# The sample's state updates as a stream of their own, behind its outputs, in a decoder layer on one core

## The chip, the cores and the metric

The kernel runs on one NeuronCore of a Trainium2 chip. The metric is the device time of one execution in microseconds (us); the median of three runs is compared, and the trace is of one profiled execution. The engines are named as in the profile: PE (TensorE, products), DVE (VectorE), ACT (ScalarE), POOL (GpSimd) and SP (SyncE, which issues the DMAs here).

## The reference

One decoder layer for 512 prompt tokens and for a sample of 8 sequences with 4 new tokens each. Its three parts are a half-step feed-forward network, a mixer and a second feed-forward network. All of it is in float32. The mixer, cut to what matters here:

```python
def token_mixer(h, pos, conv_buf, S0, attend, p):
    proj = h @ p['w_in']
    u, z, b_raw, a_raw, q_sw, k_sw, v_sw, gate_a, gate_b = jnp.split(proj, split_idx, axis=-1)
    ...
    o_dn, S_new = gated_delta_rule(q_dn, k_dn, v_dn, g, beta, S0)
    o_dn = rmsnorm(o_dn, p['dn_norm']) * jax.nn.silu(z)
    ...
    y = jax.nn.sigmoid(gate_a) * o_dn + jax.nn.sigmoid(gate_b) * o_sw
    return y @ p['w_out'], (kbuf_new, vbuf_new, conv_new, S_new)

def step(S, xs):                      # gated_delta_rule, one chunk
    v_new = un - jnp.einsum('bhcd,bhde->bhce', wn, S)
    o = (jnp.einsum('bhcd,bhde->bhce', qn * jnp.exp(gn)[..., None], S)
         + jnp.einsum('bhij,bhje->bhie', an, v_new))
    S = S * jnp.exp(g_last)[..., None] + jnp.einsum('bhcd,bhce->bhde', k_dec, v_new)
    return S, o
```

So a chunk of the delta rule gives an output `o`, from the old state, and a new state. The output goes through a norm (the inverse root of its mean square) and a gate and is added to the attention's output; the state goes to memory. Each of the 8 heads has a state of 128 x 128 floats for the prompt and eight of them, one per sequence, for the sample.

## The kernel before

The 544 tokens (512 + 32) are worked on as two halves of 272. A float32 product is made of three products of rounded parts (line 301): hi x hh, hi x hl and lo x hh, where hi and lo are the two parts of a weight block (line 270 casts hi on ACT, line 271 subtracts for lo on DVE or POOL) and hh and hl those of the activations. A unit of a projection is half of a 128-column block: 4 weight blocks of 128 x 128.

The program is written by generators. The main one feeds the projections, and each step of it adds a cost to a clock of the program's own; the side streams (`Streams`, line 145) yield a cost and a latency, and a stream's next step comes up when the clock has passed its due time (now + 1.5 x latency). Of the due streams the one of lowest priority number, then the oldest, goes first. The code order found in this way sets the order on every engine; a high-priority mark at the weight splits moves these ahead.

Four prompt streams (`delta`, two heads each) end in a root: pro (line 1369) sums squares over the partitions, twelve small DVE operations (`rsqrt`, lines 340 to 345, after one that adds the epsilon) make the inverse root ro0y, prb (line 353) spreads it over the partitions, and line 1377 multiplies the outputs od with it. These go to memory (`odd`), and `merge_stream` loads them block by block (odm, line 1548) and adds them to the attention's output osw (lines 1555, 1557). One odm tile is used for one block after another.

`delta_sample` does the sample for a group of four heads, hg = 0 and then 1. The states of its heads are tiles S0 (512 KB each). It makes the outputs (so4, line 1656, and their squares in tq), then vm, scales the states on POOL (line 1667), makes the products psu (line 1673) and adds them to the states on DVE (line 1677), two heads at a time, and stores each pair (line 1680). Then it makes the root of the sample's outputs (pro4 on line 1682, srx and sroy, prb4 on line 353), multiplies (line 1689) and merges them into osw (`merge_sample`, lines 1700 to 1704).

In `main`, w_out's first two output blocks take hh and hl of osw. Blocks 0 to 3 of osw are split when they are merged and the first head group is in, blocks 4 to 7 when the second head group is in. Then six more output blocks follow, whose split weights are kept for both halves: tiles fhw and flw of the pool fp2. The second network's last step, `Last` (line 714), needs a tile xn6, which also comes from fp2. Pools that close give their place to later ones, so a first write of a late tile waits for the last use of what lay there. In bytes per partition, S0 of the sample's pool lies at 193120 to 209504; xn6 at 132064, fhw at 156640 and flw at 181216, 24576 bytes each.

Of the kernel before, what the change touches and what calls it, by code (L numbers as in the profile page):

```python
# [10 lines left out]
F32 = mybir.dt.float32  # L11
# [8 lines left out]
P = 128  # L20
# [767 lines left out]
class Mixer:  # L788
# [455 lines left out]
    def delta(self, gi, kq, vT, dp, si):  # L1244
# [125 lines left out]
        rx = st.tile([P, M], F32, tag=f"rx{si}", name="rx", bufs=1)  # L1370
        nc.vector.tensor_scalar(out=rx, in0=prv[:, :, 0], scalar1=128.0 * EPS * EPS, scalar2=None, op0=ALU.add)
        ro = L.rsqrt(rx, [P, M], f"ro{si}")
        yield 0.85, 3.5 * L_DN
        for n in range(G):
            pb = L.wd("prb")
            L.bcast_cols(ro, [(n * NC + c, 0, P) for c in range(NC)], [pb[:, c * P:(c + 1) * P] for c in range(NC)], "ro")
# [182 lines left out]
    def delta_sample(self, hg, sp):  # L1559

        nc, L, a = self.nc, self.L, self.a
        st = L.st
        hs = slice(4 * hg, 4 * hg + 4)
        col = slice(32 + hg, 33 + hg)
        k4 = self.kqs[:, hs, 0, :]
# [91 lines left out]
        o2 = sp.tile([P, P], F32, tag="so2", name="so2")  # L1657
        nc.scalar.activation(out=o2, in_=oT, func=AF.Square, scale=128.0 ** -0.5)
        nc.vector.tensor_tensor(out=tq, in0=tq, in1=o2, op=ALU.add)
        yield 0.5, 0.6 * L_SMP  # L1660
        vm = sp.tile([P, SB, P], F32, tag="km", name="vm")
        nc.vector.tensor_tensor(out=vm, in0=vn.unsqueeze(1).to_broadcast([P, SB, P]),
                                in1=L.c("SEQM").unsqueeze(2).to_broadcast([P, SB, P]), op=ALU.mult)
        for h0 in (0, 2):
# [13 lines left out]
                yield 1.0, 0.5 * L_SMP  # L1678
            for h in hs:
                nc.sync.dma_start(out=a["delta_sample"][0, :, 4 * hg + h].rearrange("s k v -> k s v"), in_=S0[h])  # L1680
        pr = L.wk("pro4")
        nc.tensor.matmul(out=pr[:, :64], lhsT=tq, rhs=L.ones[:, :64], start=True, stop=True)
        rx = st.tile([P, 1], F32, tag="srx", name="srx")
        nc.vector.tensor_scalar(out=rx, in0=pr[:, 0:1], scalar1=128.0 * EPS * EPS, scalar2=None, op0=ALU.add)
        ro = L.rsqrt(rx, [P, 1], "sro")
        yield 0.3, 3.5 * L_SMP
        pb = L.wk("prb4")
        L.bcast_cols(ro, [(0, 0, P)], [pb[:, :P]], "sro")
        nc.vector.tensor_tensor(out=o, in0=o, in1=pb[:, :P], op=ALU.mult)
        yield 0.3, 0.3 * L_SMP  # L1690
        while any(self.z[h] is None or not self.gb_done[h] for h in range(4 * hg, 4 * hg + 4)):
            yield 0.0, 1.0 * L_SMP
        self.merge_sample(hg, o)
        self.merged[8 + hg] = True

    def merge_sample(self, hg, o):
        nc, L = self.nc, self.L
# [68 lines left out]
    def plan(self, feed):  # L1766

        L, win, x = self.L, self.win, self.x
        self.att_done = [0] * 4
        self.kqv, self.z, self.gb_done = {}, [None] * NH, [False] * NH  # L1770
        self.od_done, self.merged = [False] * NH, [False] * 10
        self.decays_done = False
        self.odd = L.dr.tile([NH, P, SEQ], F32, name="odd")
        qT, kT = (lambda: self.qT), (lambda: self.kT)
        q = lambda c: [u for b in range(8) for u in L.project(win, Q0 + b * P, x, self.evac(qT, b, (c,)), cs=(c,),
                                                              pool_lo=False)]
        self.mark0 = feed.add(q(0))
        self.marks = []

        def ba(ps):  # L1780
            self.sch.spawn(self.decays(ps, self.rp), 0)

        for n in ORDER:
            if n == "B":
                us = L.project(win, BA0, x, ba, ncol=16)
            elif n == "Q":
                us = q(1)
            elif n == "K":
                us = [u for b in range(2) for u in L.project(win, K0 + b * P, x, self.evac(kT, b))]
            elif n == "V":  # L1790
                us = [u for b in range(2) for u in L.project(win, V0 + b * P, x, self.v_block(b))]
            elif n[0] == "U":
                us = self.head_blocks(int(n[1]))
            else:
                us = self.gate_blocks(int(n[1]))
            self.marks.append((n, feed.add(us)))


def layer(ctx, tc, a, dbg=None, stop=None):
# [70 lines left out]
    def main():  # L1870
# [72 lines left out]
        fp = bufs["fp"] = L.pool("fp2", 1)  # L1943
        d = bufs["d"] = fp.tile([P, 8, T], F32, name="dacc2")

        last.append(Last(L, tmp, d, bufs["sqd"], hp, fp))
        feed.add(L.ffn("ffn2", x, bufs, NFRONT, NDOWN, lambda c: sch.spawn(last[0].finish(c, last[0].ps), 0), last[0].block))
        yield from feed.run(mo)
        while 0 not in done:
# [33 lines left out]
```

## Time and profile before

| what | us |
|---|---|
| median of 3 runs | 1587.06 (1586.16 to 1587.81) |
| the profiled execution | 1590.33 |
| its span | 1588.5 |
| PE busy | 1513.1 (95%) |
| DVE busy | 846.5 (53%) |
| ACT busy | 633.5 (40%) |
| POOL busy | 293.7 (18%) |

The span runs from the first to the last instruction that the profile shows, and the execution's own time is 1.83 us longer. Busy time is that in which an engine works on an instruction; issuing a DMA does not count. The mixer's projections, the streams and the attention lie between about 500 and 1113 us, w_out from 1089 on, the second network from about 1165.

### The profile page before, as it was taken

Reading aid. Unit: us, or ns where it says so; the run is one execution under the profiler, and the core shown is the slowest. Engines: PE = TensorE matmul, PEld = TensorE weight load, DVE = VectorE, ACT = ScalarE, POOL = GpSimd, SP = SyncE. Lnnn points to the kernel's source line nnn. Section 1 sums busy time; section 2 is a strip of 40 time slices with the busy share of each in tenths; the row PEclk is TensorE's granted clock in tenths of the full one; section 3 lists DMA queues with packets and bytes.
Section 4 is the critical chain, followed back from the end, with each engine's and each line's share of the span. In section 5 each row is a group of like instructions: output and inputs, shape, how many; then the busy total and the mean of one; then the engine's idle time right before and its main releaser. Section 6 shows DMA issues by size and latency. Waiting matters only on the chain. (4 is left out here: it accounts for less than half of the span.)

```text
span 1588.5 us, 32490 instructions
## 1 busy us (share of the span) xinstructions
PE 1513.1 (95%) x12819; PEld 1408.5 (89%) x12819; DVE 846.5 (53%) x2080; ACT 633.5 (40%) x1397; POOL 293.7 (18%) x386
## 2 busy tenths in 40 slices
PE   7999999999998999998999999998989999999996
PEld 3898999999987999898788898896979999999995
DVE  5433322333488787468879658748374332233354
ACT  4222222222445554254675432233465332233363
POOL 1000000000353232123012112312548000000042
PEclk9999999999999999799999999999999999999998
DMA  9455454554656434554212325624426323333253
GB/s 323 140 172 179 129 160 141 160 158 136 197 162 194 115 89 105 127 146 112 48 44 67 99 69 133 160 78 131 139 67 167 107 82 92 91 91 87 83 148 102
DMA packets 314533, 199.64 MB, mean 126 GB/s; under 512 B 36464, under 2 KB 297331, under 8 KB 314092
## 3 DMA queue, kind: packets, MB, share of 16 engines
q1 hardware_dynamic: 314086, 197.46, 43.7%
q8 instruction: 100, 1.64, 0.4%
q14 instruction: 53, 0.43, 0.1%
q10 hardware_dynamic: 294, 0.11, 0.0%
HBM read 182.08 MB, written 16.36 MB: 125 GB/s over the span
## 5 line engine op out<-in xcount | busy, mean ns | idle before, releaser
L270 ACT CAST hi<-raw 128x512 fp32r<-128x512 f32 (+2 forms) x502 | 287.0, 581 | 592.7 <-PE pu L301 161.8
L271 DVE TENSOR_TENSOR lo<-raw,hi 128x512 fp32r<-128x512 f32 (+2 forms) x368 | 249.9, 681 | 436.0 <-ACT hi L270 416.9
L301 PE MATMUL pb<-hh,hi 128*128 128x272 f32 (+1 forms) x1008 | 234.6, 303 | 2.2 <-ACT hh L270 1.8
L301 PE MATMUL pb<-hh,lo 128*128 128x272 f32 (+1 forms) x1008 | 226.5, 295 | 2.3 <-DVE lo L271 2.3
L301 PE MATMUL pb<-hl,hi 128*128 128x272 f32 (+1 forms) x1008 | 225.3, 294 | 0.0
L271 POOL TENSOR_TENSOR lo<-raw,hi 128x512 fp32r<-128x512 f32 (+1 forms) x104 | 139.1, 1341 | 450.9 <-ACT hi L270 423.6
L301 PEld LDWEIGHTS pb<-hh,hi 128*128 128x128 f32 (+1 forms) x1008 | 165.4, 192 | 12.1 <-issue 4.5
L301 PE MATMUL pd<-fh,hi 128*128 128x272 f32 x704 | 171.8, 291 | 0.0
L301 PE MATMUL pd<-fl,hi 128*128 128x272 f32 x704 | 170.9, 290 | 0.0
L301 PEld LDWEIGHTS pb<-hh,lo 128*128 128x128 f32 (+1 forms) x1008 | 165.0, 192 | 5.3 <-DVE lo L271 2.5
L301 PEld LDWEIGHTS pb<-hl,hi 128*128 128x128 f32 (+1 forms) x1008 | 165.2, 191 | 2.6 <-issue 1.0
L301 PE MATMUL pd<-fh,lo 128*128 128x272 f32 x672 | 162.2, 289 | 0.8 <-POOL lo L271 0.8
L301 PE MATMUL pg<-hh,hi 128*128 128x272 f32 x672 | 149.7, 293 | 7.1 <-ACT hh L550 3.4
L301 PE MATMUL pu<-hh,hi 128*128 128x272 f32 x672 | 148.8, 292 | 1.6 <-ACT hi L270 1.6
L301 PE MATMUL pg<-hl,hi 128*128 128x272 f32 x672 | 147.8, 290 | 0.8 <-DVE hl L539 0.7
L301 PE MATMUL pu<-hl,hi 128*128 128x272 f32 x672 | 146.5, 289 | 0.0
L301 PE MATMUL pu<-hh,lo 128*128 128x272 f32 x672 | 146.0, 289 | 0.0
L301 PE MATMUL pg<-hh,lo 128*128 128x272 f32 x672 | 145.8, 289 | 0.0
L301 PEld LDWEIGHTS pd<-fh,hi 128*128 128x128 f32 x704 | 120.6, 189 | 8.4 <-issue 5.9
L301 PEld LDWEIGHTS pg<-hh,hi 128*128 128x128 f32 x672 | 108.8, 189 | 19.4 <-ACT hh L550 5.4
L301 PEld LDWEIGHTS pd<-fl,hi 128*128 128x128 f32 x704 | 120.9, 189 | 0.0
L301 PEld LDWEIGHTS pu<-hh,hi 128*128 128x128 f32 x672 | 108.7, 190 | 11.2 <-issue 5.9
(445 smaller groups left out, 2508.5 us busy)
## 6 DMA issues: line engine op xcount, KB each, us to landing
raw<-w_in SPq DMA_DIRECT2D x136, 256.0 KB
wa<-w_ada SPq DMA_DIRECT2D x56, 512.0 KB
raw<-ffn_w_gate SPq DMA_DIRECT2D x94, 256.0 KB
raw<-ffn_w_up SPq DMA_DIRECT2D x94, 256.0 KB
raw<-ffn_w_down SPq DMA_DIRECT2D x92, 256.0 KB
wb<-w_ada SPq DMA_DIRECT2D x32, 256.0 KB
S<-state_delta SPq DMA_DIRECT2D x8, 512.0 KB
delta_sample<-S SPq DMA_DIRECT2D x8, 512.0 KB
```

What stands on the lines that cost most here:

```text
L270: self.nc.scalar.copy(out=hi, in_=raw)
L271: (eng or self.nc.vector).tensor_tensor(out=lo, in0=raw, in1=hi.bitcast(F32), op=ALU.subtract)
L301: self.nc.tensor.matmul(out=ps[:m, c, :TH], lhsT=a[:r, kt, :m], rhs=b[:r, kx, c * TH:(c + 1) * TH], start=first and i == 0, stop=last and ...
```

## The change

There are four edits. The step between the prompt's root and its spreading yields 4.5 in place of 3.5 units of latency. In `delta_sample`, vm and all that updates and stores the states moves to a generator of its own, `update_states`, which is spawned when the outputs are made, with priority 1; the root of the outputs then follows at once, and between root and spreading 5.0 units are yielded where 3.5 were. A flag, `updating`, holds back the second head group until the first group's updates are written. And xn6 comes from a pool of its own that is opened after fp2, so that fhw lies at 132064, flw at 156640 and xn6 at 181216, where S0 was.

```diff
@@ -1370,7 +1370,7 @@
         ro = L.rsqrt(rx, [P, M], f"ro{si}")
-        yield 0.85, 3.5 * L_DN
+        yield 0.85, 4.5 * L_DN
         for n in range(G):
@@ -1560,6 +1560,8 @@
         st = L.st
+        while self.updating:
+            yield 0.0, 1.0
         hs = slice(4 * hg, 4 * hg + 4)
@@ -1657,7 +1659,28 @@
         nc.vector.tensor_tensor(out=tq, in0=tq, in1=o2, op=ALU.add)
-        yield 0.5, 0.6 * L_SMP
+        yield 0.5, 2.0 * L_SMP
+        self.updating = True
+        self.sch.spawn(self.update_states(hg, sp, S0, E4, kdec, vn), 1)
+        pr = L.wk("pro4")
+        nc.tensor.matmul(out=pr[:, :64], lhsT=tq, rhs=L.ones[:, :64], start=True, stop=True)
+        rx = st.tile([P, 1], F32, tag="srx", name="srx")
+        nc.vector.tensor_scalar(out=rx, in0=pr[:, 0:1], scalar1=128.0 * EPS * EPS, scalar2=None, op0=ALU.add)
+        ro = L.rsqrt(rx, [P, 1], "sro")
+        yield 0.3, 5.0 * L_SMP
+        pb = L.wk("prb4")
+        L.bcast_cols(ro, [(0, 0, P)], [pb[:, :P]], "sro")
+        nc.vector.tensor_tensor(out=o, in0=o, in1=pb[:, :P], op=ALU.mult)
...
+        self.merge_sample(hg, o)
+        self.merged[8 + hg] = True
+
+    def update_states(self, hg, sp, S0, E4, kdec, vn):
+
+        nc, L, a = self.nc, self.L, self.a
+        yield 0.0, 0.5
         vm = sp.tile([P, SB, P], F32, tag="km", name="vm")
...
@@ -1678,20 +1701,7 @@
                 nc.sync.dma_start(out=a["delta_sample"][0, :, 4 * hg + h].rearrange("s k v -> k s v"), in_=S0[h])
-        pr = L.wk("pro4")
...
-        yield 0.3, 3.5 * L_SMP
...
-        self.merged[8 + hg] = True
+        self.updating = False
@@ -1769,7 +1779,7 @@
-        self.decays_done = False
+        self.decays_done = self.updating = False
@@ -1943,7 +1953,7 @@
-        last.append(Last(L, tmp, d, bufs["sqd"], hp, fp))
+        last.append(Last(L, tmp, d, bufs["sqd"], hp, L.pool("xq", 1)))
```

What this does to the order is shown at three places, all at the end of the mixer, where the second head group, the last prompt stream and w_out's first blocks meet. The numbers behind a name tell buffers apart.

PE, before: the updates' last products (psu), the sample's sum (pro) and its spreading (prb), then 48 products of w_out.

```order
L1673 MATMUL psu_13653<-vm,skdec 128x512
L1673 MATMUL psu_13654<-vm,skdec 128x512
L1673 MATMUL psu_13659<-vm,skdec 128x512
L1673 MATMUL psu_13660<-vm,skdec 128x512
L1682 MATMUL pro_13667<-ones,stq 128x64
L353 MATMUL prb_13684<-ident,sroy 128x128
```

PE, after, where the sample's root is spread; its pro stands 36 products, the prompt's prb and one pair of psu ahead of this prb, and three more groups of psu come behind it.

```order
L301 MATMUL pb<-hh,hi 128x272 x2
L301 MATMUL pb<-hl,hi 128x272 x2
L301 MATMUL pb<-hh,lo 128x272 x2
L1696 MATMUL psu_13560<-vm,skdec 128x512
L1696 MATMUL psu_13561<-vm,skdec 128x512
L353 MATMUL prb_13566<-ident,sroy 128x128
```

So pro and prb, which stood next to each other behind all updates, now stand apart, with other work between and updates behind.

DVE, before, in the same place: the last state additions (S), the start of the sample's root.

```order
L1677 TENSOR_TENSOR S_13136<-S_13136,psu_13596 128x512
L1677 TENSOR_TENSOR S_13138<-S_13138,psu_13597 128x512
L1677 TENSOR_TENSOR S_13140<-S_13140,psu_13653 128x512
L1677 TENSOR_TENSOR S_13142<-S_13142,psu_13654 128x512
L1677 TENSOR_TENSOR S_13140<-S_13140,psu_13659 128x512
L1677 TENSOR_TENSOR S_13142<-S_13142,psu_13660 128x512
L1684 TENSOR_SCALAR srx<-pro_13667 128x1
L340 TENSOR_SCALAR sroy<-srx 128x1
```

DVE, after: the root's first operations, among splits of w_out's activations (hl) and weights (lo) and the prompt's outputs (od).

```order
L271 TENSOR_TENSOR lo<-raw,hi 128x512
L1528 SCALAR_TENSOR_TENSOR z<-tg,pb 128x544
L1668 TENSOR_SCALAR srx<-pro_13485 128x1
L271 TENSOR_TENSOR hl<-osw,hh 128x544
L340 TENSOR_SCALAR sroy<-srx 128x1
L271 TENSOR_TENSOR hl<-osw,hh 128x544
L341 TENSOR_SCALAR sroy<-sroy 128x1
L271 TENSOR_TENSOR hl<-osw,hh 128x544
L271 TENSOR_TENSOR lo<-raw,hi 128x512
L343 SCALAR_TENSOR_TENSOR sroa<-srx,sroy 128x1
L271 TENSOR_TENSOR hl<-osw,hh 128x544
L344 TENSOR_TENSOR sroa<-sroa,sroy 128x1
```

Behind these rows the two od products and the rest of the root follow, and no state addition stands ahead of it any more.

DVE, after, a little later: the sums for blocks 6 and 7 of osw (odm, osw) and the splits that need them, among the state additions.

```order
L1555 SCALAR_TENSOR_TENSOR odm<-odm,cwT,z 128x512
L1700 TENSOR_TENSOR S_13116<-S_13116,psu_13619 128x512
L1557 TENSOR_TENSOR osw<-osw,odm 128x512
L1700 TENSOR_TENSOR S_13118<-S_13118,psu_13620 128x512
L271 TENSOR_TENSOR hl<-osw,hh 128x544 x3
L1700 TENSOR_TENSOR S_13120<-S_13120,psu_13684 128x512
L1555 SCALAR_TENSOR_TENSOR odm<-odm,cwT,z 128x512
L1700 TENSOR_TENSOR S_13122<-S_13122,psu_13685 128x512
L1557 TENSOR_TENSOR osw<-osw,odm 128x512
L1700 TENSOR_TENSOR S_13120<-S_13120,psu_13690 128x512
L1700 TENSOR_TENSOR S_13122<-S_13122,psu_13691 128x512
L271 TENSOR_TENSOR flw<-raw,fhw 128x512 x4
```

Before, both blocks' sums stood ahead of the root, and here they come behind it, with two state additions ahead of block 7's multiply and one before its sum.

SP, before: the stores of the prompt's outputs (odd), the loads of blocks 6 and 7 (odm), the four state stores, and xT, the residual for the second network.

```order
L1379 DMA odd<-od 128x512 x2
L1548 DMA odm<-odd 128x512
L279 DMA raw<-w_out 128x4x128 x2
L1548 DMA odm<-odd 128x512
L279 DMA raw<-w_out 128x4x128
L1680 DMA delta_sample<-S_13136 128x8x128
L1680 DMA delta_sample<-S_13138 128x8x128
L1680 DMA delta_sample<-S_13140 128x8x128
L1680 DMA delta_sample<-S_13142 128x8x128
L279 DMA raw<-w_out 128x4x128 x4
L1940 DMA xT_13707<-xsp 128x4352
L279 DMA raw<-w_out 128x4x128 x3
```

SP, after, in the same place.

```order
L1379 DMA odd<-od 128x512 x2
L279 DMA raw<-w_out 128x4x128
L1548 DMA odm<-odd 128x512
L1703 DMA delta_sample<-S_13116 128x8x128
L1703 DMA delta_sample<-S_13118 128x8x128
L1548 DMA odm<-odd 128x512
L1703 DMA delta_sample<-S_13120 128x8x128
L1703 DMA delta_sample<-S_13122 128x8x128
L279 DMA raw<-w_out 128x4x128
L1950 DMA xT_13707<-xsp 128x4352
L279 DMA raw<-w_out 128x4x128 x6
```

The load of block 7 has moved behind the first two state stores, all four stores ahead of one w_out load instead of four, and six w_out loads stand behind xT where three stood.

## Rows read from the trace of the kernel before

**Rows 1.** The head of the profile's page.

```profile
span 1588.5 us, 32490 instructions
```

**Rows 2.** Waits of PE, 1040 to 1120: engine, line, releaser, us, times, longest.

```profile
PE prb L353 <- DVE sroy L345: 3.6, 1, 3.6
PE prb L353 <- DVE ro0y L345: 2.3, 1, 2.3
PE pb L301 <- ACT hh L270: 1.8, 1, 1.8
```

**Rows 3.** Windows: us, busy us of PE, PEld, DVE, ACT, POOL; PEclk, DMA share, GB/s.

```profile
1078.00:1080.00 2.00, 0.75 (x7) 0.78 (x8) 1.39 (x3) 0.27 (x1) 2.00 (x2) 1.00 0.00 0
1080.00:1100.00 20.00, 19.36 (x135) 15.98 (x133) 16.50 (x25) 5.60 (x11) 4.90 (x4) 1.00 0.47 145
1104.00:1106.00 2.00, 0.71 (x3) 0.71 (x4) 1.26 (x4) 1.41 (x3) 0.00 (x0) 0.50 0.34 100
1110.00:1112.00 2.00, 2.00 (x17) 1.89 (x16) 2.00 (x5) 1.24 (x2) 0.00 (x0) 1.00 0.98 277
```

**Rows 4.** Timeline of PE: start, us, line, operation, count, idle before and releaser.

```profile
1079.25 1.06 PE L353 MATMUL prb<-ident,ro0y 128*128 128x128 f32 x8 [2.32 <-DVE ro0y L345]
...
1082.24 0.37 PE L301 MATMUL pb<-hh,hi 128*128 128x272 f32 x1
...
1088.43 1.13 PE L1673 MATMUL psu<-vm,skdec 32*128 32x512 f32 x4
...
1096.95 1.99 PE L1673 MATMUL psu<-vm,skdec 32*128 32x512 f32 x8
...
1098.92 0.44 PE L1682 MATMUL pro<-ones,stq 128*128 128x64 f32 x2
...
1102.99 0.45 PE L353 MATMUL prb<-ident,sroy 128*128 128x128 f32 x1 [3.63 <-DVE sroy L345]
...
1105.29 1.27 PE L301 MATMUL pb<-hh,hi 128*128 128x272 f32 x4 [1.85 <-ACT hh L270]
...
1113.43 0.29 PE L301 MATMUL pb<-hh,fhw 128*128 128x272 f32 x1
```

**Rows 5.** Timeline of DVE, 1075 to 1107.

```profile
1075.40 1.83 DVE L344 TENSOR_TENSOR ro0a<-ro0a,ro0y 128x8 f32<-128x8 f32 x1
...
1085.27 1.98 DVE L271 TENSOR_TENSOR hl<-osw,hh 128x544 fp32r<-128x544 f32 x3
...
1090.27 1.21 DVE L1534 SCALAR_TENSOR_TENSOR z<-tg,z 128x544 f32<-128x544 f32 x1
...
1092.43 0.75 DVE L1555 SCALAR_TENSOR_TENSOR odm<-odm,cwT,z 128x512 f32<-128x512 f32 x1 [0.35 <-DMA odm<-odd]
...
1098.18 2.48 DVE L1677 TENSOR_TENSOR S<-S,psu 128x512 f32<-128x512 f32 x4 [3.08 <-PE psu L1673]
...
1100.58 0.15 DVE L1684 TENSOR_SCALAR srx<-pro 128x1 f32<-128x1 f32 x1
...
1106.55 3.58 DVE L271 TENSOR_TENSOR flw<-raw,fhw 128x512 fp32r<-128x512 f32 x4
```

**Rows 6.** Timeline of POOL: the sample's states are scaled.

```profile
1075.30 7.53 POOL L1667 TENSOR_TENSOR S<-S,sgrow 128x1024 f32<-128x1024 f32 x4 [5.84 <-PE pks L1638]
```

**Rows 7.** Timeline of SP's DMA queue: issues.

```profile
1012.41 1.01 SPq L1680 DMA_DIRECT2D delta_sample<-S  x2
...
1015.77 2.76 SPq L1623 DMA_DIRECT2D S<-state_delta  x2
...
1089.78 0.34 SPq L1548 DMA_DIRECT2D odm<-odd  x1
```

**Rows 8.** Timeline of ACT: the first casts of the kept weights.

```profile
1105.69 2.69 ACT L270 CAST fhw<-raw 128x512 fp32r<-128x512 f32 x5
```

**Rows 9.** Waits of PE, 640 to 1040, two of the list.

```profile
PE pkq L1288 <- DVE so L1215: 2.5, 1, 2.5
...
PE psc L1010 <- DVE vs L1307: 2.2, 1, 2.2
```

More of the change, by code (lines that the diff above doesn't have):

```diff
@@ L1659, in delta_sample @@
         nc.vector.tensor_tensor(out=tq, in0=tq, in1=o2, op=ALU.add)
-        yield 0.5, 0.6 * L_SMP
+        yield 0.5, 2.0 * L_SMP
[10 more added lines that the diff above has]
+        nc.vector.tensor_tensor(out=o, in0=o, in1=pb[:, :P], op=ALU.mult)
+        yield 0.3, 0.3 * L_SMP
+        while any(self.z[h] is None or not self.gb_done[h] for h in range(4 * hg, 4 * hg + 4)):
+            yield 0.0, 1.0 * L_SMP
+        self.merge_sample(hg, o)
[3 more added lines that the diff above has]
+        yield 0.0, 0.5
         vm = sp.tile([P, SB, P], F32, tag="km", name="vm")
@@ L1680, in delta_sample @@
                 nc.sync.dma_start(out=a["delta_sample"][0, :, 4 * hg + h].rearrange("s k v -> k s v"), in_=S0[h])
-        pr = L.wk("pro4")
[L1682 to L1685, printed above, removed]
-        yield 0.3, 3.5 * L_SMP
[L1687 to L1693, printed above, removed]
-        self.merged[8 + hg] = True
+        self.updating = False
     def merge_sample(self, hg, o):
```

## Prediction

> **What bounds the kernel now.** I read the list of TensorE's waits first, then the timelines of the stretch that the list points to, then the same stretch in windows for the granted clock. TensorE sets the end of this kernel: nearly all of its 1588.5 us [rows 1] it is busy, and so the time that can move is its waits and its slow clock. In the last stretch before w_out's kept blocks, from 1040 to 1120, it waits three times: 2.3 us for the prompt's root (ro0y), 3.6 us for the sample's root (sroy) and 1.8 us for hh [rows 2]. The timeline shows the reason of the last two. The psu products of the sample's state update, 1.99 us, are the last thing before pro, the sum for the sample's root, and nothing but that root is queued behind pro: prb starts 3.63 us after it and the next projection product 1.85 us after that [rows 4]. VectorE spends the first part of this on the four state additions, 2.48 us, and only then starts the root's twelve operations, 1100.58 to 1102.99, 0.2 us each [rows 5]. The first wait has another cause: one operation of the prompt's root takes 1.83 us [rows 5] while GpSimd scales the states, four operations in 7.53 us [rows 6]; the same chain runs at 0.2 us an operation without that.
>
> A second loss lies under the third wait. The granted clock is 0.50 at 1104 to 1106, that is 1.2 GHz, where it was 1.00 (2.4 GHz) from 1078 to 1080 [rows 3]. So the 48 products behind prb take 8.14 us, 1105.29 to 1113.43, where 48 of the same form took 6.19 us, 1082.24 to 1088.43, 0.129 us each [rows 4]: 1.95 us lost.
>
> **What the change takes away.** The three waits are 2.32 + 3.63 + 1.85 = 7.80 us, the clock 1.95 us: 9.75 us is the ceiling. In the changed order the prompt's prb stands behind 48 products (6.2 us) after its pro, so the root's held operations lie beside products. The sample's pro stands 36 products, the prompt's prb and a pair of psu ahead of its own prb, and the state updates lie between products, so nothing has to be awaited at the end but the split of the late blocks. No operation is added or dropped: the same products, additions, stores. That the first write of the kept weights (fhw) no longer waits for the four state stores is needed for this: with the tile in its old place it would wait for the last of them, which now comes later.
>
> **What is late next.** Three things, counted from the order of the change and durations of before.
>
> The sample's root. Between pro and its prb TensorE has 36 products (4.64 us), the prompt's prb (1.06) and a psu pair (1.13) [rows 4]: 6.8 us. VectorE has in the same place, in its new order, the root's twelve operations (2.4 us) mixed with four hl splits at 0.66, one weight split and two od products of about that size [rows 5]: 7.0 us, and ahead of the root's first operation one more split and a z, about 1.4 us more, which start when the prompt's root is through. So sroy is late by 8.4 - 6.8 = 1.6, with the pick-up 1.7 us. Bounds: 0 if VectorE gets there early, 3.5 if GpSimd's scaling holds one operation more (1.83 us [rows 5, 6]). I take 1.7.
>
> Block 7. Counted from sroy: VectorE has a state addition (0.62), z (1.21), another addition (0.62), then the sample's merge. In before, prb to the first following product took 2.30 us with merge and one cast [rows 4]; without the cast (0.54 [rows 8]), the product itself (0.45) and the first pick-up, which the additions hide, about 1.1. Then block 6's merge and two additions (0.75 + 0.62 + 0.7 + 0.62): 6.2 us. Only then does the second store go, and the load of block 7 (odm) stands behind both stores on SyncE's queue: issued at about 6.9. In before this load was used 2.65 us after its issue, 1089.78 to 1092.43 [rows 5, 7], with no store ahead of it. Of a pair of such stores issued at 1012.41 and about 0.5 later, each was awaited by the load of a new state: the first load went out at 1015.77, 3.36 us after its store, the second about 2.3 us later in the same row [rows 7], some 5.2 us after its own. Behind the second store, issued at 6.4, I put its end 4.2 later (between 3.36 and 5.2) and odm's landing 0.7 after that, at 11.3, not at 6.9 + 2.65 = 9.55. From there: its multiply, an addition, the sum (2.1) make 13.4; five fhw casts, which now wait for that sum, 2.69 [rows 8], 16.1; hh of block 7, 16.7. TensorE has from sroy on: prb 0.3, 12 products 1.55, psu 1.13, 36 products 4.64, psu 2.26 and 31 of the last 48 products 4.0, together 13.9. So it waits 2.8 us; nine products later, at 17.85, it wants hl of block 7, which stands behind two additions (1.24) and four flw splits (3.58 [rows 5]), at 18.9: 1.05 more. Sum 3.85, bounds 1 (the load lands as in before, and only the splits are late) and 6.5 (it lands 2.7 us later still).
>
> By the Trainium skill, "DMA: Bandwidth & Descriptors", section "Queues, rings and completion order", descriptors are consumed in ring order on each of the transfer engines, though completion need not follow the order of issue. By that the load does come after the stores' data, and the term is the 3.85 as taken; if it could pass them it would be about 1.75 smaller.
>
> The clock. The new waits are 1.7, 2.8 and 1.05 us, with work between. The wait of 2.32 us at 1076.9 left the clock at 1.00 [rows 3, 4]; 3.63 and 1.85 on top of each other brought 0.50. The new ones are nearer to the first, so I take 0.5 of the 1.95 us, bounds 0 and 1.95. The Trainium skill, "TensorE: Matmul & The Clock Gate", section "What's actually happening", has the slow clock as the default state, which activity releases; read strictly, each pause is a chance to lose it, and the sum would carry the whole 1.95, a gain of 2.25 instead of 3.7.
>
> Costed at nothing: the six w_out loads that now stand behind the large xT load, where three did. A unit of kept weights is 12 products, 1.55 us, so the first of the six is wanted 9.3 us after the first fhw product. xT goes when hl of block 7 is made, about 1.4 us before that product; its 2.2 MB at the 277 GB/s of 1110 to 1112 [rows 3] take 8 us, load and split of the next unit about 2 more: 8.6 after the product, 0.7 to spare. If that cover is gone it costs up to 1.5. The first head group (hg 0) has the same new order, but many products between its steps, and in the list of 640 to 1040 its root is no wait; nothing there either, as for the roots of the three earlier prompt streams, which move back by up to 14 products with no product waiting for what they make. The products, transposes and scores of the stretch after the first of these roots are reshuffled, though: two waits stand there now, pkq 2.5 and psc 2.2 [rows 9], which may go, stay or double. I put 0, with 3 to either side.
>
> **The sum.** 9.75 - 1.7 - 3.85 - 0.5 = 3.7 us off the profiled execution's 1590.33, 1586.6. That execution is 3.27 above the median of 1587.06, so in the median 1583.4 us. A difference of about 0.2%, 3.2 us, is what a measurement of this kernel can tell from no change: faster means under 1583.9, slower over 1590.2.
>
> **Rivals.** *The whole ceiling.* VectorE gets through its list in time and block 7's load lands early: 9.75 us, 1577.3. For it: each late term is worked out from a list in which VectorE runs without a gap, and it is 1 to 2 us at a time. Against: VectorE has nothing to spare there, 16.5 us of the 20 from 1080 to 1100 [rows 3], and the load does stand behind the stores.
>
> *The gain is given back at block 7.* The casts of fhw now wait for the sum of block 7, and hh and hl of that block for them. With the landing 2.7 us later and the clock at half again, 9.75 - 1.7 - 6.5 - 1.95 leaves nothing: 1587. For it: the last wait of the chain is a DMA behind 1 MB of stores, and the transfer engines are full when they are used: 277 GB/s at a share of 0.98 from 1110 to 1112 [rows 3]. Against: the pair of rows 7 bounds the stores' ends, and 2.7 us more would be another store's time.
>
> *Slower, by the reshuffled middle.* The place is the stretch from the first prompt root on, some 700 to 745. VectorE is the engine that TensorE waits for there, and PSUM slots are freed by its copies. The two waits of rows 9 show what one costs, 2.5 and 2.2 us. The new order puts one pkq pair and the transposes of vT behind more products, and the chain that needs them later runs with less ahead. It decides the sign if 7 us of new waits appear, three of that size: four cost 9.4, 1592.8 in the median. For it: three later prompt streams and the first head group are shifted as well. Against: what moved there moved by some ten products, and a wait is as likely to go.
>
> *The change does not do what it says.* If updates stayed ahead of the root, the time would not move; the order shows pro ahead of all psu, so this has no chance of its own.
>
> **How the numbers follow.** Forecast, gain 1.5 to 7: 0.50. Whole ceiling: 0.12. Given back, within 3 us of no change: 0.23. Slower: 0.15. Of the forecast's half 0.38 lies beyond 3.2 us, 0.12 below. Faster 0.38 + 0.12 = 0.50, same 0.12 + 0.23 = 0.35, slower 0.15. The range goes from the ceiling, 1577.3, to 1589.8, and leaves out the slower case and a little below.
>
> **What would show it.** In the changed kernel's profile: no wait of prb for ro0y; a wait of the sample's prb for sroy of 1 to 3 us, before the last 96 products; a wait for hh of block 7 with a cast behind fhw and a DMA wait of odm's multiply behind it; a clock at or near 1.00 in the stretch before the first fhw product, which comes some 3 to 5 us earlier against the end of the last w_in product. It is wrong if the waits of 700 to 1000 grow by more than 3 us together, if the odm load is used well after 5 us from its issue, or if the sample's prb waits 4 us as before.

## The result, and the profile after

| | before | changed |
|---|---|---|
| median of 5 runs, beside each other (lowest to highest) | 1587.81 us (1586.16 to 1589.83) | 1597.86 us (1596.14 to 1604.25) |
| ratio | | 1.0076, 95% interval 1.0054 to 1.0097 |
| the profiled execution | 1590.33 | 1596.14 |
| its span | 1588.5 | 1594.4 |
| PE busy | 1513.1 | 1518.0 |

The changed kernel is slower by 10 us, beyond the range. The end of the mixer, on which the forecast rested, looks much as forecast, but for the clock. These are TensorE's waits there, with the columns of [rows 2]:

```profile
PE pb L301 <- ACT hh L270: 3.5, 1, 3.5
PE prb L353 <- DVE sroy L345: 1.9, 1, 1.9
PE pro L1666 <- DVE ro0y L345: 1.3, 1, 1.3
```

The waits of [rows 2] were 7.8 us together, these are 6.7. The wait for the prompt's root is gone, that for sroy has halved, that for hh has doubled, and one of 1.3 is new. TensorE's timeline has them in place, as [rows 4] before:

```profile
1087.75 0.41 PE L1666 MATMUL pro<-ones,stq 128*128 128x64 f32 x2 [1.34 <-DVE ro0y L345]
...
1091.05 1.03 PE L353 MATMUL prb<-ident,ro0y 128*128 128x128 f32 x8
...
1096.55 0.29 PE L353 MATMUL prb<-ident,sroy 128*128 128x128 f32 x1 [1.90 <-DVE sroy L345]
...
1113.32 0.82 PE L301 MATMUL pb<-hh,hi 128*128 128x272 f32 x2 [3.48 <-ACT hh L270]
...
1117.79 0.43 PE L301 MATMUL pb<-hh,fhw 128*128 128x272 f32 x1
```

The new wait goes with GpSimd's scaling of the states [rows 6], which now runs beside other work of VectorE. POOL's timeline, as in [rows 6]:

```profile
1077.79 8.97 POOL L1690 TENSOR_TENSOR S<-S,sgrow 128x1024 f32<-128x1024 f32 x4 [0.44 <-PE pks L1640]
```

VectorE's timeline beside it:

```profile
1079.97 2.16 DVE L271 TENSOR_TENSOR lo<-raw,hi 128x512 fp32r<-128x512 f32 x1
1082.05 2.93 DVE L1685 TENSOR_TENSOR vm<-svn,cst 128x1024 f32<-128x1024 f32 x1
1084.91 0.15 DVE L1371 TENSOR_SCALAR rx<-pro 128x8 f32<-128x8 f32 x1
1085.10 1.69 DVE L340 TENSOR_SCALAR ro0y<-rx 128x8 int32<-128x8 int32 x1
...
1087.32 0.28 DVE L1661 TENSOR_TENSOR stq<-stq,so 128x128 f32<-128x128 f32 x1
```

Beside the scaling a split takes 2.16 us (0.69 elsewhere) and one operation of the prompt's root 1.69 (the next take 0.17). The sample's squares, stq, stand behind these, and TensorE's pro, now early in its queue, waits for stq. (The row names ro0y, the operation that ended last before pro; pro reads stq, which ended at 1087.60.)

For block 7, SP's issues:

```profile
1101.74 1.59 SPq L1703 DMA_DIRECT2D delta_sample<-S  x2
1103.42 0.73 SPq L1548 DMA_DIRECT2D odm<-odd  x1
```

VectorE's timeline, when the load has come:

```profile
1107.91 0.75 DVE L1555 SCALAR_TENSOR_TENSOR odm<-odm,cwT,z 128x512 f32<-128x512 f32 x1 [2.04 <-DMA odm<-odd]
...
1109.17 0.69 DVE L1557 TENSOR_TENSOR osw<-osw,odm 128x512 f32<-128x512 f32 x1
```

ScalarE's casts, which wait for that sum:

```profile
1110.02 2.70 ACT L270 CAST fhw<-raw 128x512 fp32r<-128x512 f32 x5 [7.02 <-DVE osw L1557]
1112.62 0.64 ACT L270 CAST hh<-osw 128x544 fp32r<-128x544 f32 x1
```

The load of block 7 is used 4.49 us after its issue, behind two stores, where [rows 5, 7] had 2.65 without any. The Trainium skill, "DMA: Bandwidth & Descriptors", section "Queues, rings and completion order", has descriptors consumed in ring order on each transfer engine; the trace agrees with that at 4.49 us. The changed kernel's load ahead of this one, with no store before it, was used 3.12 us after its issue.

So the end wins a little and gives most of it back. The loss lies earlier, as the experiments will show. The windows of the whole stretch from the first prompt root to the kept weights show where. The columns are those of [rows 3]; each row is a stretch of 60 to 200 us, and (1 - PEclk) x length is called the clock lost in it (an upper count, since TensorE may idle in part of a slow stretch). Before:

```profile
690.00:800.00 110.00, 101.64 (x971) 90.92 (x969) 90.89 (x299) 58.72 (x167) 24.50 (x48) 0.97 0.37 93
800.00:1000.00 200.00, 192.57 (x2013) 173.86 (x2011) 151.31 (x503) 95.00 (x267) 45.65 (x73) 0.99 0.33 84
1000.00:1060.00 60.00, 58.52 (x675) 53.58 (x676) 40.03 (x97) 18.04 (x43) 12.71 (x14) 1.00 0.52 139
1060.00:1130.00 70.00, 62.20 (x556) 57.68 (x555) 40.17 (x77) 27.71 (x58) 26.38 (x23) 0.95 0.51 154
```

Changed:

```profile
690.00:800.00 110.00, 99.45 (x937) 85.87 (x936) 87.92 (x293) 57.20 (x165) 19.82 (x43) 0.97 0.35 85
800.00:1000.00 200.00, 194.28 (x2007) 175.30 (x2007) 149.05 (x500) 93.46 (x263) 42.10 (x69) 0.98 0.33 83
1000.00:1060.00 60.00, 57.34 (x605) 50.91 (x605) 34.66 (x87) 14.76 (x33) 10.30 (x11) 0.89 0.47 128
1060.00:1130.00 70.00, 63.28 (x567) 59.01 (x566) 41.52 (x83) 26.09 (x56) 22.74 (x20) 0.95 0.44 135
```

TensorE's busy time hardly differs, but busy at half the clock does half the work. Summed over windows of 2 us, for more digits, 690 to 1130 lost 8.5 us of clock before and 17.0 changed; counting only the time in which TensorE is busy, 7.1 and 15.9. As anchors, take the first product of the first root's pro (same place in both orders), by the view of line 1369, of before:

```profile
L1369 PE MATMUL pro<-ones,tq x64: 217/275/289, 693.6 to 1073.1; 128*128 128x64 f32 x64
```

and changed:

```profile
L1369 PE MATMUL pro<-ones,tq x64: 217/275/323, 686.3 to 1082.6; 128*128 128x64 f32 x64
```

The other anchor is the first product with kept weights, 1113.43 [rows 4] and 1117.79. Between them lie 419.8 us before and 431.5 changed: 11.7 more, of which 8.5 are clock and 3.2 the rest. The waits do not explain it: from 690 to 1000 they sum to 15.3 us before and 16.0 after. Over their whole span, though, the two profiled executions lost the same, 30.6 us each (mean clock 0.981 in both): before lost 11.9 of it ahead of 690, changed 3.4. The 5.9 us between their spans are 4.9 of busy and 1.0 of idle time. So this pair alone does not show that the change costs clock; the means over many runs do. Beside the experiments these kernels ran 103 and 16 times, and each run's mean clock gives 26.6 us lost before and 34.5 changed, and a time without it of 1560.7 and 1564.9. So 8 of the 12 us between the means are clock, and 4 the rest.

### The profile page after: what moved, and what is told of

Its sections match the earlier page's. It is cut to its first block, busy times and chain, and to the rows that moved or that the text cites. A ratio compares the mean times of both kernels' runs of the same rounds, so it can differ in the third digit from the quotient of the medians.

```text
span 1594.4 us, 32494 instructions
## 1 busy us (share of the span) xinstructions
PE 1518.0 (95%) x12819; PEld 1410.1 (88%) x12819; DVE 844.2 (53%) x2080; ACT 634.8 (40%) x1397; POOL 288.5 (18%) x386
## 5 line engine op out<-in xcount | busy, mean ns | idle before, releaser
L271 POOL TENSOR_TENSOR lo<-raw,hi 128x512 fp32r<-128x512 f32 (+1 forms) x104 | 135.5, 1305 | 474.4 <-ACT hi L270 460.6
```

Of the source, the lines that this page charges most:

```text
L271: (eng or self.nc.vector).tensor_tensor(out=lo, in0=raw, in1=hi.bitcast(F32), op=ALU.subtract)
```

## The experiments

All kernels in one table. "Early root" is the 4.5 for the roots of the first prompt streams, "hg 0 stream" the update stream for the first head group. "Lost" is the clock lost in a run, (1 - mean clock) x span, mean of its runs; "rest" is the mean time less this. The last two columns are from the one profiled execution: from the first root's pro to the first kept product, and the clock lost from 690 to 1130, of that. In e4 the first kept product stands at another place in the order. The row of the changed kernel holds g4's runs too.

| kernel | early root | hg 0 stream | ratio to before (interval) | lost | rest | pro to kept | lost there |
|---|---|---|---|---|---|---|---|
| before | - | - | 1 | 26.6 | 1560.7 | 419.8 | 8.5 |
| h3 before again | - | - | one run | | | 420.2 | 10.2 |
| changed | yes | yes | 1.0076 (1.0054 to 1.0097) | 34.5 | 1564.9 | 431.5 | 17.0 |
| g4 changed again | yes | yes | 1.0072 (1.0048 to 1.0095) | | | 429.4 | 15.3 |
| e1 root only | yes | - | 1.0035 (1.0018 to 1.0052) | 33.1 | 1559.6 | 425.6 | 15.4 |
| e2 tile only | - | - | 1.0053 (1.0030 to 1.0077) | 32.3 | 1563.1 | 428.0 | 12.0 |
| e3 stream only | - | yes | 1.0041 (1.0023 to 1.0060) | 27.9 | 1565.2 | 421.8 | 8.5 |
| e4 stream and tile | - | yes | 1.0003 (0.9981 to 1.0025) | 27.4 | 1560.2 | | 1.7 |
| f1 first three roots | yes | yes | 1.0073 (1.0046 to 1.0100) | 34.0 | 1563.3 | 428.7 | 17.1 |
| f2 last root | - | yes | 1.0014 (0.9996 to 1.0032) | 27.1 | 1562.5 | 423.3 | 10.2 |
| f3 late stores | yes | yes | 1.0075 (1.0048 to 1.0103) | 30.9 | 1566.8 | 430.6 | 17.1 |
| f4 last root, late stores | - | yes | 1.0025 (1.0007 to 1.0043) | 27.0 | 1562.1 | 421.9 | 12.0 |
| g1 second group | yes | - | 1.0037 (1.0015 to 1.0060) | 34.6 | 1559.2 | 430.7 | 20.5 |
| g2 second group, root 3.5 | - | - | 1.0014 (0.9991 to 1.0037) | 32.0 | 1557.7 | 421.9 | 12.0 |
| g3 first root | yes | yes | 1.0084 (1.0051 to 1.0117) | 32.3 | 1568.6 | 436.1 | 20.5 |
| h1 spaced | yes | yes | 1.0105 (1.0072 to 1.0139) | 42.8 | 1562.0 | 432.0 | 20.5 |
| h2 second group, last root | - | - | 1.0009 (0.9983 to 1.0034) | 29.5 | 1560.3 | 424.7 | 15.4 |

**The parts apart.** e1 is the kernel before with the later root alone, e2 with the late tile alone, e3 with the stream alone, e4 with stream and tile.

```diff
 e1
-        yield 0.85, 3.5 * L_DN
+        yield 0.85, 4.5 * L_DN
 e2
-        last.append(Last(L, tmp, d, bufs["sqd"], hp, fp))
+        last.append(Last(L, tmp, d, bufs["sqd"], hp, L.pool("xq", 1)))
 e3: update_states as in the change, neither of these two; e4: the same with e2's line
```

> Only the prompt root's latency is raised from 3.5 to 4.5, all else as before. Theory A (the reshuffled middle from 690 us on makes the change slow): slower by 5 to 10 us (ratio 1.003 to 1.006), with waits for the attention's softmax (ppt, pkt) of 2 us and more between 690 and 800 as in the changed kernel. Theory B (the updates as a stream make it slow, in the first head group and at the end): faster by 1 to 3 us (0.998 to 0.9995), since the 2.3 us wait for ro0y at the end goes and the middle only trades waits.

> Only the tile xn6 gets its own pool, all else as before. Both theories: the same within 0.2% (0.998 to 1.002). The casts of the kept weights may run before the last state stores are through, but they were waited for by nothing but the 1.85 us wait for hh; at most 2 us faster.

> The updates as a stream of their own, with the tile and the prompt root's latency as before. Theory A: no slower than before (0.997 to 1.001). Theory B: slower by 5 to 12 us (1.003 to 1.008), with waits for stq and psu between 1000 and 1030, a half clock after them, and the casts of the kept weights waiting for the last state store at the end.

> The changed kernel but for the prompt root's latency, which stays at 3.5. Theory A: the same as before or faster by up to 4 us (0.997 to 1.001). Theory B: as slow as the changed kernel, 1.005 to 1.009, with the same waits between 1000 and 1030 and for hh of block 7 at the end.

The later root alone costs 0.35%, and its rest (1559.6) is no worse than before's (1560.6 in the runs beside it): the whole loss is clock, 33.1 us against 26.2. The tile alone costs 0.53%, which I had not expected; its lost clock is up too, to 32.3, with no early root. Waits of e2 at the end of the mixer:

```profile
PE prb L353 <- DVE sroy L345: 8.7, 1, 8.7
PE prb L353 <- DVE ro0y L345: 2.3, 1, 2.3
PE pro L1682 <- DVE S L1677: 2.3, 1, 2.3
PE pb L301 <- ACT hh L270: 1.8, 1, 1.8
```

With fhw free early, its splits are ready before the sample's root and go ahead of it on VectorE, so sroy is awaited for 8.7 us. The stream alone has its own price. e3 came out in theory B's range, with the wait at the end that B named, but with no half clock between 1000 and 1050:

```profile
PE pb L301 <- ACT dacc L1899: 10.3, 1, 10.3
PE pro L1666 <- DVE ro0y L345: 1.3, 1, 1.3
PE prb L353 <- DVE sroy L345: 0.5, 1, 0.5
```

There the sroy wait is nearly gone, and the kept weights' place, still under the states, is awaited for 10.3 us in one piece. Tile and stream need each other, as the prediction had it. Together (e4) they cut these waits to 4.3 us in all, and the time is still that of before.

**Which root.** f1 has the later root for the first three streams, f2 for the last, g3 for the first alone; the rest is the change.

```diff
-        yield 0.85, 4.5 * L_DN
+        yield 0.85, (4.5 if gi < 3 else 3.5) * L_DN     # f1; f2: gi == 3; g3: gi == 0
```

> The changed kernel with the prompt root's latency at 4.5 for the first three prompt streams and 3.5 for the last. Theory A (the three earlier roots reshuffle the middle, and that is the loss): as slow as the changed kernel, ratio 1.005 to 1.009, with waits of ppt and pkt of 2.5 us and more between 690 and 800. Theory B (the last root delays the prompt's outputs and so block 7 of osw at the end): 0.998 to 1.002, with no wait for hh over 1.5 us at the end.

> The changed kernel with the latency at 4.5 for the last prompt stream alone and 3.5 for the first three. Theory A: 0.997 to 1.001, with the middle's waits as in the kernel before (about 15 us from 690 to 1000). Theory B: 1.004 to 1.009, with the wait for hh of block 7 at 3 us and more.

> The changed kernel with the latency at 4.5 for the first prompt stream alone. If the first root's move is what makes the two waits of 2.8 (ppt) and 2.6 us (pkt) in the attention and the later half clocks: 1.004 to 1.009, both waits there. If the second and third root do it: 0.999 to 1.003, the waits as in the kernel before.

The last root, the one the forecast was made for, is nearly harmless: 1.0014, a little above theory A's range, with an interval that holds 1. The first alone brings the whole loss: 1.0084. Between f2 and f1, which ran side by side, lie 7.6 us in the mean, 6.9 of them clock. f1's waits at the end, 3.3 us, are lower than the changed kernel's 6.7, and it is no faster.

**The stores.** f3 holds the second group's stores until all eight prompt blocks are merged, f4 does that with the last root alone late.

```diff
-            for h in hs:
+            for h in hs if hg == 0 else ():
                 nc.sync.dma_start(...)
+        while hg == 1 and not all(self.merged[:8]):
+            yield 0.0, 0.5
+        for h in range(4) if hg == 1 else ():
+            nc.sync.dma_start(...)
```

> The changed kernel with the second head group's state stores held back until all eight blocks of osw are merged, so that the last load of the prompt's outputs does not stand behind them. Theory A: still slower than before, 1.003 to 1.007; the wait for hh at the end falls from 3.5 us to 1.5 or less, worth 2 to 3 us. Theory B: most of the loss goes, 0.999 to 1.003.

> Both: latency 4.5 for the last prompt stream alone, and the state stores of the second head group held back. Theory A: the fastest of the four, 0.995 to 0.999. Theory B: 0.999 to 1.004, no faster than the kernel without the later root.

In f3 the wait for hh is 1.5 us where it was 3.5, 0.7 for hl comes up, and the time stays (1.0075). That need not be the stores' doing. One of them still goes out ahead of the load (1100.36, the load 1100.96), and g4, the changed kernel again with its stores in place, has this at the end:

```profile
PE pb L301 <- ACT hh L270: 1.3, 1, 1.3
PE pb L301 <- DVE hl L271: 0.5, 1, 0.5
```

In f3 and g4 alike the clock fell earlier, behind the wait for sroy, so TensorE came later to block 7. In g4, where the first profile shows 1.00 at the same distance from that wait (1098 to 1100):

```profile
1104.00:1106.00 2.00, 2.00 (x8) 1.36 (x8) 1.31 (x4) 0.51 (x1) 0.15 (x1) 0.50 0.53 146
```

f4, expected to be the fastest of all, came at 1.0025 and is no test of the stores: two still go out ahead of the load (1091.16, the load 1092.44), as in f2, and the load is used 5.1 us after its issue in both. So what the load's place behind the stores costs is not shown by f3 and f4. That block 7 is not the loss is shown by f2, which has 2.3 us of wait for hh and 1.1 for hl there and yet no loss that can be told.

**Which head group.** g1 runs the updates of hg 0 in line and with the latencies as before, with the stream for hg 1 only; g2 is g1 with all roots at 3.5.

```diff
-        yield 0.5, 2.0 * L_SMP
+        yield 0.5, (2.0 if hg == 1 else 0.6) * L_SMP
...
-        self.sch.spawn(self.update_states(hg, sp, S0, E4, kdec, vn), 1)
+        if hg == 1:
+            self.sch.spawn(self.update_states(hg, sp, S0, E4, kdec, vn), 1)
+        else:
+            yield from self.update_states(hg, sp, S0, E4, kdec, vn)
...
-        yield 0.3, 5.0 * L_SMP
+        yield 0.3, (5.0 if hg == 1 else 3.5) * L_SMP
```

> The changed kernel with the update stream for the second head group alone; the first group updates its states ahead of its root, as before. Theory A1 (the later roots and the first group's update stream together thin out the projection products from 1020 to 1045, and the clock falls there): no half clock between 1020 and 1050, and 3 to 6 us faster than the changed kernel, 1.002 to 1.006. Theory A2 (the loss is made in the attention and the solves, 690 to 1000, by the later roots alone): as slow as the changed kernel, 1.005 to 1.009.

> The same with the prompt root's latency at 3.5 for all streams, so that only the second head group's updates and the tile differ from the kernel before. Both theories: 0.996 to 1.000; the middle as before, about 15 us of waits from 690 to 1000 and 2 from 1000 to 1045, and less than the 7.7 us of waits at the end. If it is 1.001 or more, the end gains nothing even without the middle's loss.

> The changed kernel itself, once more, beside the others on one chip: 1.005 to 1.010, mean granted clock 0.977 to 0.980 against 0.983 of the kernel before, and the half clock near 1030 to 1045 again in its profile if it belongs to the order and not to chance.

g1 costs what e1 costs, 0.37%, by the clock (34.6 lost), as theory A1 had it. g2, by its expectation a gain, came at 1.0014: nothing that can be told, and no gain of the end. g4 came as expected, 1.0072, with half clock at 1038 to 1046. So the loss has two parts. The first is the early root. In five pairs that differ by it (e1 and before, the change and e4, f1 and f2, f3 and f4, g1 and g2; f1 and f2 differ in the last root too) it costs 4 to 12 us in the mean, of which 7, 7, 7, 4 and 3 are clock. The smallest is g1 less g2, 2.6 us with a standard error of 1.7, an estimate from the runs' clocks: g2 lost 32.0 without any early root. So a run's lost clock does not hang on this root alone. The second part is hg 0's stream on top of that root. g4 less g1, side by side, is 5.7 us, all of it in the rest (1565.3 and 1559.2). Without the early root the stream costs no time: e4 less g2 is -2.2 us, 2.5 more in the rest and 4.7 less of clock.

**The stretch of hg 0.** In the changed kernel VectorE has a block's merge (z, odm) ahead of the solve's copies XL and X, for which two pairs of psu wait. DVE's timeline:

```profile
1022.20 1.42 DVE L1534 SCALAR_TENSOR_TENSOR z<-tg,z 128x544 f32<-128x544 f32 x1 [3.71 <-ACT tg L1513]
1023.66 0.78 DVE L1555 SCALAR_TENSOR_TENSOR odm<-odm,cwT,z 128x512 f32<-128x512 f32 x1
1024.36 1.26 DVE L1462 TENSOR_TENSOR XL<-XL,pt 32x256 f32<-32x256 f32 x3
1025.66 1.71 DVE L1464 TENSOR_TENSOR X<-X,pz 32x256 f32<-32x256 f32 x4
```

PE's timeline, the two pairs:

```profile
1025.77 1.09 PE L1696 MATMUL psu<-vm,skdec 32*128 32x512 f32 x2 [0.39 <-DVE XL L1462]
1027.42 1.12 PE L1696 MATMUL psu<-vm,skdec 32*128 32x512 f32 x2 [0.56 <-DVE X L1464]
```

The same stretch in windows:

```profile
1024.00:1026.00 2.00, 1.61 (x13) 1.42 (x12) 1.94 (x5) 0.00 (x0) 0.00 (x0) 1.00 1.04 256
1026.00:1028.00 2.00, 1.44 (x4) 0.33 (x3) 1.93 (x5) 0.00 (x0) 0.00 (x0) 1.00 0.06 12
1028.00:1030.00 2.00, 2.00 (x26) 1.34 (x25) 2.00 (x5) 0.36 (x1) 0.95 (x1) 0.96 0.00 0
1030.00:1032.00 2.00, 2.00 (x21) 1.94 (x19) 0.89 (x5) 0.37 (x1) 0.00 (x0) 0.50 0.83 247
```

Two waits of under 0.6 us, and from about 1030 to 1044 the granted clock is at 0.50 (1.2 GHz): 6.8 us lost. Half clock in this stretch stands in all six profiles with both early root and hg 0's stream (1.7 to 6.8 us) and in none of the other eleven. In the five of the six that do not space the group's products the 0.56 us wait for X stands there, and the clock falls within 3 us behind it. The four with the stream but no early root (e3, e4, f2, f4) have neither the wait nor the fall. h1 spaces the group's products out to see whether they cause it; h2 drops both early parts; h3 is the kernel before, profiled again.

```diff
-                yield 1.0, 0.5 * L_SMP
+                yield 1.0, (3.0 if hg == 0 else 0.5) * L_SMP      # h1
 h2: g1 with
+        yield 0.85, (4.5 if gi == 3 else 3.5) * L_DN
```

> The changed kernel, with the update products of the first head group further apart: each step of its stream yields 3.0 units of latency where 0.5 stood; everything else is as in the change, all four prompt roots late. Theory (the group's psu pairs, which follow one another with short waits and few products between, pull the clock down at 1029 to 1046): no stretch at clock 0.50 there, 3.4 to 6.8 us back, a ratio to before near 1.004. Rival A (the loss comes from the later roots alone, wherever the update products stand): still 1.007, with or without the half clock at that place. Rival B (the later first root costs clock at 903 to 970 too, as in six of seven profiles with it): half-clock pieces stay there, so the ratio does not come below 1.003.

> The update stream for the second head group only, with the late tile and the sample's early root, and the later prompt root for the last prompt stream only: the parts of the change that touch the end of the mixer, and none that touches what is before it. Theory (the change's loss comes from the earlier places, and its end of the mixer gains what the waits there show, 2 to 4 us, unless the clock takes it back): 0.998 to 1.000. Rival (the end of the mixer gives back all that it wins): 1.0015, as with the last root late in the whole change.

> The kernel before, profiled once more, for a second look at where its clock falls. If the stretch at half clock near 655 to 673 in its first profile belongs to its order, it is there again, 6.8 to 8.5 us long; if such stretches come by chance, their place or length differs. No half clock at 1029 to 1046 is expected by either, since the other kernels without both the early later root and the first group's stream show none there.

h1 missed its mark: 1.0105 is slower than its theory and both rivals had it. The psu waits are gone and TensorE is shown busy without a gap, and still the clock falls, for less long:

```profile
1028.00:1030.00 2.00, 2.00 (x20) 0.87 (x18) 1.26 (x2) 0.36 (x2) 0.00 (x0) 1.00 0.55 128
1030.00:1032.00 2.00, 2.00 (x10) 1.81 (x10) 0.69 (x1) 0.00 (x0) 0.00 (x0) 0.64 0.36 105
1032.00:1034.00 2.00, 2.00 (x29) 1.75 (x29) 0.00 (x0) 1.24 (x2) 0.08 (x1) 0.51 0.00 0
```

The second group, held until the first is written, comes late in turn (the last of its pks at 1084.9, 1077.5 in the changed kernel), and h1's end of the mixer pays for it. Two of its waits there:

```profile
PE prb L353 <- DVE sroy L345: 8.1, 1, 8.1
PE pro L1666 <- DVE stq L1661: 2.4, 1, 2.4
```

Beside them 10.2 us of clock are lost from 1095 to 1116. So h1 neither clears nor convicts the psu waits: 1.7 us of half clock in place of 3.4 to 6.8 speaks for a share in it, the rest does not come from them. h2 shows that the edits at the end, alone, gain nothing that can be told: 1.0009, and not the 0.998 to 1.000 of its theory at the median. h3 has 6.8 us of half clock at 656 to 671, near the 8.5 at 655 to 673 of the first profile of before. But of the changed kernel's two profiles one has none at 600 to 690 and the other 8.5. One program does both, which is chance, and single profiles have to be read so.

The table's last column shows more than that chance. The eight profiles with an early root lost 15.3 to 20.5 us of clock from 690 to 1130 (mean 17.9), the nine without lost 1.7 to 15.4 (mean 10.0), so the two groups just touch. The eight's extra loss does not lie in one place: 800 to 1000 has 5.1 against 2.1 in the mean, 1000 to 1060 has 2.8 against 0, 1060 to 1130 has 5.8 against 4.2.

## Why the prediction was wrong, step by step

- *What bounds the kernel.* The waits were read rightly, but clock only where a wait stood on it, 1.95 us. In before's profile 30.6 us are lost to the clock over the whole span, four times the three waits. That the clock outside the tail could move was in no term.
- *The prompt's root.* Its prb no longer waits, as forecast. The prediction read one held operation in before, and there were two, 1.83 us each (1075.40 and 1077.27). Beside GpSimd's scaling VectorE's operations went on taking longer, and the sample's pro waits 1.34 us behind them. I had put the held operation beside products, and the sample's squares behind it nowhere: a missing term of 1.3.
- *The sample's root.* 1.7 forecast, 1.90 measured, in part by luck: VectorE's list took 7.6 us and not 8.4 (1088.82 to 1096.41), but began 0.9 us later than counted, since the prompt's root was late.
- *Block 7.* From sroy, at 1096.55, the load was to go out at 6.9 (measured 1103.42, 6.87), to be used at 11.3 (1107.91, 11.36), the casts to start at 13.4 (1110.02, 13.47) and hh to be made at 16.7 (1113.26, 16.71). TensorE came 0.6 us earlier than counted, so the wait is 3.48, not 2.8; the wait for hl that was to follow (1.05) did not come, since the split was through at 1115.17 and TensorE, at half clock, was not yet past the products before it. 3.85 forecast, 3.48 measured. The chain held to a tenth of a microsecond in this profile, with luck in it: the 4.2 us for the store's end was chosen between 3.36 and 5.2. In g4, the same program, the load was used at 12.3, hh was made at 17.7, and the waits are 1.35 and 0.52, the second being the one for hl that did not come here.
- *The clock at the end.* I took 0.5 of 1.95 as still lost, by nearness to the wait of 2.32. The clock fell as before: the half-clock stretch at 1111 to 1119 counts 3.4 us of lost clock, as much as the one at 1102 to 1110 before, and in g4 one of the same size stands at 1103 to 1111. The term was sized by a single draw. h3, the kernel before again, has the same wait of 2.32 us, and half clock behind it; its prb took 1.94 us and not 1.06:

```profile
1076.80 1.94 PE L353 MATMUL prb<-ident,ro0y 128*128 128x128 f32 x8 [2.32 <-DVE ro0y L345]
```

Of seven profiles with a wait of 2.3 to 2.5 us at this place five show half clock behind it, and two (before and e2) do not. The Trainium skill, "TensorE: Matmul & The Clock Gate", section "What's actually happening", has the slow clock as the default state, which activity releases; the trace agrees, in that the clock is at 0.50 behind a wait in both profiles of the changed kernel (1112 to 1118, in g4 1104 to 1110). Its strict reading in the prediction, which kept the whole 1.95, came nearer here; that each pause loses the clock no run shows.
- *The sum for the end.* Waits 7.8 less 6.7, 1.1 us, and no clock. h2 and f2 (1.0009 and 1.0014, with intervals that hold 1) agree that the end is worth nothing that can be told.
- *Costed at nothing.* This is the step that failed, with its 0 and 3 to either side: the roots of the three earlier prompt streams and the new order of hg 0. Together they cost 8 us of clock and 4 of the rest. The earlier roots cost 7.6 us between f2 and f1, hg 0's order 5.7 between g1 and g4. I had asked whether a product waits for what the root makes, and none does; what the shift does to the granted clock over 400 us I did not ask. The w_out loads behind xT, costed at nothing too, did cost nothing: from the first kept product to 1165 no wait of TensorE is for a weight.
- *The rivals.* The whole ceiling did not come. Of what "given back at block 7" needed, the half clock came and the later landing did not. "Slower, by the reshuffled middle" had the sign and the cause, the earlier roots, at 0.15. Its mechanism is not what happened: it wanted 7 us of new waits at 700 to 745, and the waits of 690 to 1000 grew by 0.7. pkq 2.5 and psc 2.2 of [rows 9] did go, and these came in their place:

```profile
PE ppt L1052 <- ACT s L1040: 4.4, 3, 2.8
PE pkt L1306 <- DVE mx L1017: 2.6, 1, 2.6
```

- *What would show it wrong.* None of the three signs came: waits of 700 to 1000 up by less than 3 us, odm used 4.49 us after its issue, prb waiting 1.9. A list of signs that holds only waits cannot show a loss that is not a wait.

Shown: the early root costs time in each of the five pairs that differ by it, and over the five more by clock (27 us) than by the rest (11); hg 0's stream adds to it, and no cost of it is seen without that root. The kernels without that root and without a wait of 8 us or more at the end (e4, f2, f4, g2, h2) lie within 0.25% of before. Open: by what the later root lowers the clock at so many places, where the 4 us of the rest lie, and why e2 and g2 lose 32 us of clock without it. The short waits near 1026 are at most a part (h1), and no order that moves the solve's copies alone, with all else in place, was tried.

## What to carry to other kernels

Before a shift in order is costed at nothing because nobody waits for what moved, read the granted clock over the whole stretch that it reshuffles, since an engine shown as busy may be at half speed. Here the mean of runs lost 8 us more of clock, while TensorE's idle time in the two profiles grew by 1.0 (75.4 to 76.4). Make an edit for the one place it is meant for: in the changed kernel 4.5 for the last stream alone cost nothing that can be told (1.0014), the same number for all four 1.0076. Where edits free a place and move the work that fills it, time them together, since each alone can cost more than both.

## What was not expected of the hardware

Runs of one program spread over 20 us, and that goes mostly with the clock. The 103 runs of the kernel before lie between 1579.95 and 1600.19; their standard deviation is 4.2 us, and 2.0 once each run's lost clock is taken off. Single stretches at half clock cost 1.7 to 8.5 us and come and go at the same place in the same program. A profile is one draw of that.

Some of VectorE's operations beside GpSimd's scaling took about 1.5 us longer than usual, whatever their size: 1.69 us for 128 x 8 elements, 2.16 for 128 x 512, where 0.17 and 0.69 are usual. Others beside it did not: rx took its 0.15 at 1084.91 and sR its 0.29 at 1077.88, and both read a product's result. Why some are held and others not, no run here takes apart.
